# Odd mixer: the HGRN2 gate product right behind the latent queries, and the HGRN2 half of the closing product ahead of the GLA transposes

## The chip, the cores and the metric

One core of a Trainium2 chip runs the whole program. The metric is device time in microseconds. The kernel before takes 1820.97 us (median of 3 runs, 1820.81 to 1821.23). The core's engines are TensorE (PE, with its weight loads as PEld), VectorE (DVE), ScalarE (ACT), GpSimd (POOL) and SyncE (SP), whose queue issues nearly all DMAs.

## The reference

A backbone of two layers for 256 latent tokens of width 1024, with a context of 256 tokens that runs through the same weights. Layer 0 mixes by FFT and by a long convolution; layer 1, the odd layer, by two chunked linear-attention scans: GLA in raster order and HGRN2 in column order, each in both directions. Around the mixer stand two SwiGLU FFNs; each sub-layer is modulated and closed by `x <- LN(alpha*x + gate*f(x))`. The change is in the odd mixer, cut here to what matters:

```python
u = h @ w_in                    # qc kc vc rc af ab | qd ffl fbl idd gd
lat_gla, lat_hg, r, g = features(h);  ctx_gla, ctx_hg, rc, gc = features(hc)
o_gla, _ = _scan_two_way(lat_gla, ctx_gla, False)
o_hg, _ = _scan_two_way(tuple(to_col(a) for a in lat_hg), ctx_hg, False)
yg = _rms_heads(o_gla, gla_g) * silu(r)
yh = _rms_heads(from_col(o_hg) * sigmoid(g), hg_g)
y = concatenate([yg, yh]) @ w_out
```

`g`, the HGRN2 readout gate, is one product of the latent tokens with 512 columns of `w_in`. `y @ w_out` sums over eight feature blocks: in the kernel's order the first four are HGRN2's, the last four GLA's.

## The kernel before, in words

Tokens stand in four tiles of 128: 0 and 1 latent, 2 and 3 context. The features of all four, transposed and split in a high and a low fp32r part, are the eight tiles `hT`. A weight unit of 128 x 1024 floats comes by one DMA into a `raw` slot (three slots); ScalarE casts its high part (L78), VectorE subtracts the low part (L79), and TensorE does three products, high by high, low by high and high by low. The class `Stream` (L41 to L91) does this a few units ahead; `queue_odd` (L1111) lists the mixer's units in the order of use, and `g_(name, default)` reads the table of numbers G0 (L97).

No scheduler orders the work: each engine runs its instructions in the order in which the Python program records them. Between groups of matmuls the program calls `step(n)`, which records n pieces of the background queue `bg`; `flush()` records all of it. `due(t)` records the late transposes, modulation and split of token tile t for `hT` (normalisation `xn` at L398, transposes `ptr` at L411, modulation `hm` at L430, casts `hT` at L226).

In `odd_mixer` (L1119) come, in this order:

- Six latent query products in `fm_lat` (L1147): four of HGRN2 (`qh`, L1160) and two of GLA (`qg`, L1169), of 24 matmuls of 256 columns each. `due(2)` stands after the first, `flush()` behind the fourth, `due(3)` after the fifth.
- The low-rank decay product `pab` (L1183) with all four token tiles, and the feature-major units of forget gates and keys for all tokens.
- `tm_group` (L1408): the token-major products V1 and then V0, each 4 weight units by 4 token tiles, so 16 tile units with a `step(1)` behind each. During V0 `states` (L1316) of HGRN2 pair 1 run: transposes `pt`, `pb` (L1324), their copies `kT` (L1327), and two pieces later the products `pu` (L1339). `scores` (L1352) with masking by `copy_predicated` (L1372) and the sum `am` (L1376), and `outputs` (L1379) into `OH` and `OG`, follow.
- The readout gate `gg`: a `tm_group` of 2 token tiles, 8 tile units with `step(2)` behind each, which carries the scores and outputs of HGRN2 pair 2 as its filler. `permute` (L1417) brings it to column order by DMA.
- `readout(0, 4)` (L1486): the GLA gate `rc` of tile 0 with four pieces per unit, then Silu, the products `rg` by the norm's gain, `flush()`, and then `norm_og(0)`, the transposes of `OH` in `to_yt` (L1506) and of `OG` tile 0 in `og_yt(0)` (L1516).
- `close_latents` (L1628): the closing product of tile 0, k = 0 to 7 with two halves of three matmuls (L460 to L462) and `step(1)` after each k; then `readout(1, 1)`, the OG half of tile 1, and the rest.

Of the kernel before, what the change touches and what calls it, by code (L numbers as in the profile page):

```python
# [18 lines left out]
P = 128  # L19
D = 1024  # L20
KD = D // P
# [81 lines left out]
def g_(n, d):  # L103
    SEEN[n] = G0.get(n, d)
    return G.get(n, G0.get(n, d))
# [23 lines left out]
def kernel(ctx: ExitStack, tc: tile.TileContext, a, out, stop=None):  # L129
# [14 lines left out]
    def S(shape, dt=F32, name="s"):  # L144
        count[0] += 1
        return sp.tile(shape, dt, tag="s", name=f"{name}{count[0]}")
# [9 lines left out]
    def PS(name="ps"):  # L156
        count[0] += 1
        return ps.tile([P, 512], F32, tag="ps", name=f"{name}{count[0]}")
# [7 lines left out]
    def step(n=1):  # L166
        for _ in range(n):
            while bg:
                try:
                    next(bg[0])  # L170
                    break
                except StopIteration:
                    bg.pop(0)

    def flush():
        while bg:
            step()

    def run(*gens):
        for g in gens:  # L180
            for _ in g:
                pass

    def run_some(g, n):
        for _ in range(n):
            next(g, None)

    def chain(*gens):
        for g in gens:
            yield from g  # L190

    def zipped(*gens):
        gens = list(gens)
        while gens:
            for g in list(gens):
                try:
                    next(g)
                except StopIteration:
                    gens.remove(g)
            yield  # L200
# [253 lines left out]
    def due(t):  # L454
        if t in pend:
            run(pend.pop(t))
# [71 lines left out]
    def tm_mm(y, w, kp, t):  # L528

        for kk in range(2):  # L530
            k = 2 * kp + kk
            c = slice(512 * kk, 512 * kk + 512)
            x = hT[k][:, :, P * t:P * t + P]
            for n in range(2):
                pe.matmul(y, lhsT=x[:, n], rhs=w[0][:, c], start=n + k == 0, stop=False)
        for kk in range(2):
            k = 2 * kp + kk
            pe.matmul(y, lhsT=hT[k][:, 0, P * t:P * t + P], rhs=w[1][:, 512 * kk:512 * kk + 512], start=False, stop=k == KD - 1)
# [571 lines left out]

    def queue_odd():  # L1111
        for f in range(17):
            ws.add(a["od_fm"][f], f != 6, f < g_("SPN", 4), g_(f"qoi{f}", int(f in (1, 3, 4) or f > 5 and f % 2 == 1)))
        for n in range(4):
            for kp in range(4):
                ws.add(a["od_tm"][n, kp], True, n == 3, g_(f"qot{n}{kp}", kp % 2))
        for k in range(KD):
            ws.add(a["od_out"][P * k:P * k + P, :], True, k < 5, g_(f"qoo{k}", int(k < 5)))

    def odd_mixer():  # L1120
# [26 lines left out]
        def fm_lat(n):  # L1147
# [6 lines left out]
            step(n)  # L1154
            return o

        qs = S([P, 4, L], name="qh")
        for i in range(4):
            o = fm_lat(g_(f"o{i}", 2))
            act.copy(scan_view(qs[:, i]), raster(o))  # L1160
            if i == g_("od2", 0):
                due(2)
            if i == g_("of", 3):
                flush()
        q[1], q[2] = qs[:, 0:2], qs[:, 2:4]
        q[0] = S([P, 2, L], name="qg")
        for i in range(2):
            o = fm_lat(2)
            act.activation(q[0][:, i], o, AF.Copy, scale=0.125)  # L1169
            due(3)  # L1170
        az = []
        for i in range(2):
            z = S([P, 2, 512], name="az")
# [229 lines left out]
        def attend(j, tt):  # L1403
            yield from scores(j, tt)
            yield
            yield from outputs(j, tt)

        def tm_group(tiles, n):  # L1408
            y = {t: PS("tm") for t in tiles}
            for kp in range(4):  # L1410
                w = ws.get()
                for t in tiles:
                    tm_mm(y[t], w, kp, t)
                    step(n)
            return y

        def permute(dst, src):  # L1417
            for r in range(4):
                for w in range(2):
                    p0 = 64 * (r % 2) + 32 * w  # L1420
                    sy.dma_start(out=dst[r:P:4, w, :], in_=src[p0:p0 + 32, r // 2, :])


        bg.extend([zipped(operands(0, j), operands(1, j)) for j in (1, 2)])
        y = tm_group(range(NT), 1)
# [7 lines left out]
        OG = S([P, 2, 512], name="OG")  # L1433
        OH = S([P, 2, 512], name="OH")
        bg.append(zipped(operands(0, 0), operands(1, 0)))
        for j in (1, 2):
            bg.append(zipped(states(0, j), states(1, j)))
            bg.extend([attend(j, tt) for tt in range(2)])
        y = tm_group(range(NT), 1)
        gl_, gc_ = (S([P, 2, 512], name="vg") for _ in range(2))  # L1440
        for t in range(2):
            act.copy(gl_[:, t], y[t])
# [22 lines left out]
        def norm_og(t):  # L1465
            return norm_heads(OG, t, lambda h: rg[:, t, P * h:P * h + P])

        bg.extend([scores(0, 0), zipped(states(0, 0), states(1, 0)), scores(0, 1), outputs(0, 0)])
        y = tm_group(range(2), 2)
        gg = S([P, 2, 512], name="gg")  # L1470
        for t in range(2):
            act.copy(gg[:, t], y[t])
        gq = S([P, 2, 512], name="gp")
        permute(gq, gg)

        def hg_gate(tt):
            act.activation(gq[:, tt], gq[:, tt], AF.Tanh, scale=0.5)
            yield
            dve.tensor_scalar(gq[:, tt], gq[:, tt], 0.5, 0.5, op0=ALU.mult, op1=ALU.add)
            dve.tensor_tensor(OH[:, tt], OH[:, tt], gq[:, tt], op=ALU.mult)  # L1480
            yield

        rest = list(bg)
        bg.clear()
        bg.append(zipped(chain(*rest), chain(zipped(*[chain(hg_gate(t), norm_heads(OH, t, lambda h: gn[:, 1])) for t in range(2)]))))
        w = {}  # L1486

        def readout(t, n):

            y = PS("rc")  # L1490
            for kp in range(4):
                if kp not in w:
                    w[kp] = ws.get(ws.pos + 4 - kp)
                tm_mm(y, w[kp], kp, t)
                step(n)
            act.activation(rg[:, t], y, AF.Silu)
            dve.tensor_tensor(rg[:, t].rearrange("p (h v) -> p h v", h=4), rg[:, t].rearrange("p (h v) -> p h v", h=4),
                              gn[:, 0:1].to_broadcast([P, 4, P]), op=ALU.mult)

        readout(0, 4)  # L1500
        ws.split_to(ws.pos + 2)
        flush()
        Y = [S([P, 2, 2, L], F32R, name="yt") for _ in range(4)]

        def to_yt(k, o):

            for f in range(2):
                pt = PS("pt")
                for tt in range(2):
                    pe.transpose(pt[:, P * tt:P * tt + P], o[:, tt, P * (k + f):P * (k + f) + P], ident)  # L1510
                yh, yl = Y[k // 2][:, f, 0], Y[k // 2][:, f, 1]
                act.copy(raster(yh), scan_view(pt[:, 0:L]))
                dve.tensor_tensor(raster(yl), scan_view(pt[:, 0:L]), raster(yh).bitcast(F32), op=ALU.subtract)
                yield
# [7 lines left out]
                split(y[:, :, 0], y[:, :, 1], pt[:, 256 * n:256 * n + 256].rearrange("p (f t) -> p f t", f=2))  # L1522
            yield

        run(norm_og(0), to_yt(0, OH), to_yt(2, OH), og_yt(0))

        def rest():

# [1 line left out]
            w.clear()  # L1530
            hT.clear()

        return Y, outputs(0, 1), rest, chain(norm_og(1), iter([None] * 3)), og_yt(1)


    def queue_ffn_lat(l, i):
        for c in range(11):
# [87 lines left out]
                [slice(0, 512), slice(512, 768), slice(768, 1024)])  # L1625
        flush()

    def close_latents(Y, out1, rest, norm1, yt1, nxt):  # L1628


        ln = []
        run(load_ln(ln, 1, 1, GATE_ROW[1, 5], 1))
        g, b, gates = ln
        first = ws.pos
        limit = first + KD
        while limit < len(ws.units) and ws.units[limit][2]:
            limit += 1
        w, y = {}, {t: [PS("y"), PS("y")] for t in range(2)}

        def mm(t, k, h):  # L1640
            hh, hl = (Y[k // 2][:, k % 2, i, P * t:P * t + P] for i in range(2))
            c = slice(512 * h, 512 * h + 512)
            mm3(y[t][h], hh, hl, w[k][0][:, c], w[k][1][:, c], k == 0, k == KD - 1)

        bg.append(out1)
        for k in range(KD):
            w[k] = ws.get(limit)
            for h in range(2):
                mm(0, k, h)
            step(1)  # L1650
            ws.split_to(first + (4, 5, 6, 7, 7, 8, 9, 9)[k])
        flush()
        key[0] = "m1"
        bg.append(close(0, y[0], gates[0], g, b, ALPHA, EPS, nxt, True))
        rest()
        run(norm1)
        for i, (h, k) in enumerate([(h, k) for h in range(2) for k in range(4)]):
            mm(1, k, h)
            if i % 2:
                step(1)  # L1660
                ws.split_to(first + 10 + i // 2)
        run(yt1)
        for i, (h, k) in enumerate([(h, k) for h in range(2) for k in range(4, 8)]):
            mm(1, k, h)
            if i % 2:
                step(1)
        flush()
        bg.append(close(1, y[1], gates[0], g, b, ALPHA, EPS, nxt, True))
        step(1)
# [336 lines left out]
```

## Time and profile before

| | us |
|---|---|
| median of 3 runs | 1820.97 (1820.81 to 1821.23) |
| the profiled execution, whole | 1818.72 |
| its span | 1816.9 |
| TensorE busy in the span | 1735.9 (96%) |
| VectorE busy | 1253.7 (69%) |
| ScalarE busy | 716.6 (39%) |
| GpSimd busy | 254.7 (14%) |
| HBM read | 308.38 MB, 172 GB/s over the span |

The mean granted TensorE clock is 0.983. The profile is of one execution on one core: busy times are sums over instructions, the span is from the first instruction to the last. The busy shares are averages over stages with different limits; a wait is read in its stage. The odd mixer lies at about 1370 to 1640 us of the span.

### The profile page before, as it was taken

Reading aid. Unit: us, or ns where it says so; the run is one execution under the profiler, and the core shown is the slowest. Engines: PE = TensorE matmul, PEld = TensorE weight load, DVE = VectorE, ACT = ScalarE, POOL = GpSimd, SP = SyncE. Lnnn points to the kernel's source line nnn. Section 1 sums busy time; section 2 is a strip of 40 time slices with the busy share of each in tenths; the row PEclk is TensorE's granted clock in tenths of the full one; section 3 lists DMA queues with packets and bytes.
Section 4 is the critical chain, followed back from the end, with each engine's and each line's share of the span. In section 5 each row is a group of like instructions: output and inputs, shape, how many; then the busy total and the mean of one; then the engine's idle time right before and its main releaser. Section 6 shows DMA issues by size and latency. Waiting matters only on the chain. (4 is left out here: it accounts for less than half of the span.)

```text
span 1816.9 us, 21949 instructions
## 1 busy us (share of the span) xinstructions
PE 1735.9 (96%) x8212; PEld 1406.3 (77%) x8212; DVE 1253.7 (69%) x1819; ACT 716.6 (39%) x1049; POOL 254.7 (14%) x273
## 2 busy tenths in 40 slices
PE   7999999999999999999999999999998999869998
PEld 5788888877766788888887788888877778647887
DVE  6688887687688777676477677743577594656756
ACT  5532223453323442332335423333355463344443
POOL 1323311011000111111001111111011250110000
PEclk9999999999999999999999999999999999889999
DMA  9545765653124055554655455435554223535664
GB/s 330 211 180 198 254 236 213 239 177 132 71 74 158 24 201 213 188 186 173 221 187 168 165 216 201 174 102 199 197 178 145 93 82 108 162 114 208 212 211 135
DMA packets 91595, 315.10 MB, mean 173 GB/s; under 512 B 10849, under 2 KB 11585, under 8 KB 91489
## 3 DMA queue, kind: packets, MB, share of 16 engines
q1 hardware_dynamic: 86048, 297.29, 47.0%
q0 software_dynamic: 4576, 15.91, 2.7%
q8 instruction: 64, 1.05, 0.2%
q10 hardware_dynamic: 864, 0.51, 0.1%
q14 instruction: 43, 0.34, 0.1%
HBM read 308.38 MB, written 4.24 MB: 172 GB/s over the span
## 5 line engine op out<-in xcount | busy, mean ns | idle before, releaser
L79 DVE TENSOR_TENSOR wlo<-raw,whi 128x1024 fp32r<-128x1024 f32 x331 | 415.4, 1259 | 305.1 <-ACT whi L78 297.8
L78 ACT CAST whi<-raw 128x1024 fp32r<-128x1024 f32 x331 | 345.3, 1051 | 268.5 <-PE y L494 97.9
L243 DVE SCALAR_TENSOR_TENSOR mt<-mraw,cb 128x1024 bf16<-128x1024 f32 x256 | 309.6, 1249 | 3.0 <-DMA mraw<-in_mod_w_dram 3.0
L469 PE MATMUL pu<-hT,whi 128*128 128x512 f32 x1152 | 274.3, 390 | 0.0
L469 PEld LDWEIGHTS pu<-hT,whi 128*128 128x128 f32 x1152 | 215.8, 188 | 46.5 <-issue 1.0
L494 PE MATMUL y<-whi,hh 128*128 128x512 f32 x924 | 229.8, 390 | 2.9 <-ACT whi L78 2.9
L469 PE MATMUL pa<-hT,whi 128*128 128x512 f32 x960 | 228.3, 390 | 0.0
L469 PEld LDWEIGHTS pa<-hT,whi 128*128 128x128 f32 x960 | 179.6, 188 | 38.4 <-issue 0.9
L494 PEld LDWEIGHTS y<-whi,hh 128*128 128x128 f32 x924 | 172.5, 188 | 40.4 <-ACT whi L78 5.0
L226 ACT CAST hh<-sa 128x256 fp32r<-128x256 f32 x120 | 42.8, 404 | 312.1 <-DVE sa L640 312.1
L227 POOL TENSOR_TENSOR hh<-sa,hh 128x256 fp32r<-128x256 f32 x120 | 86.3, 740 | 515.9 <-ACT hh L226 484.6
L469 PE MATMUL pu<-hT,wlo 128*128 128x512 f32 x576 | 142.4, 389 | 0.4 <-DVE wlo L79 0.4
L469 PEld LDWEIGHTS pu<-hT,wlo 128*128 128x128 f32 x576 | 108.0, 188 | 23.2 <-DVE wlo L79 0.8
L494 PE MATMUL y<-wlo,hh 128*128 128x512 f32 x462 | 124.5, 391 | 0.2
L469 PE MATMUL pa<-hT,wlo 128*128 128x512 f32 x480 | 118.6, 389 | 0.0
L234 POOL TENSOR_TENSOR rstd<-rp,mhalf 128x1 f32<-128x1 f32 x42 | 36.5, 873 | 507.6 <-DVE rp L233 504.6
L79 DVE TENSOR_TENSOR lo<-raw,hi 128x1024 fp32r<-128x1024 f32 x63 | 80.4, 1290 | 38.5 <-ACT hi L78 37.9
L469 PEld LDWEIGHTS pa<-hT,wlo 128*128 128x128 f32 x480 | 90.1, 188 | 18.7
L494 PEld LDWEIGHTS y<-wlo,hh 128*128 128x128 f32 x462 | 86.6, 188 | 19.3 <-DVE wlo L79 1.5
L640 DVE TENSOR_TENSOR sa<-sa,pu 128x512 f32<-128x512 f32 x60 | 41.0, 683 | 58.0 <-PE pu L469 37.4
L78 ACT CAST hi<-raw 128x1024 fp32r<-128x1024 f32 x63 | 64.9, 1053 | 29.4 <-DMA raw<-in_ffn_out_dram 17.3
L562 PE MATMUL hd<-hi,hT 128*128 128x512 f32 x256 | 68.3, 416 | 6.5 <-ACT hT L226 3.7
(412 smaller groups left out, 2301.7 us busy)
## 6 DMA issues: line engine op xcount, KB each, us to landing
raw<-in_ffn_out_dram SPq DMA_DIRECT2D x154, 512.0 KB, 4.2
mraw<-in_mod_w_dram SPq DMA_DIRECT2D x144, 512.0 KB, 5.1
raw<-in_ffn_in_dram SPq DMA_DIRECT2D x120, 512.0 KB, 3.8
raw<-in_ffn_tm_dram SPq DMA_DIRECT2D x44, 512.0 KB, 3.3
raw<-in_od_fm_dram SPq DMA_DIRECT2D x17, 512.0 KB, 3.4
raw<-in_od_tm_dram SPq DMA_DIRECT2D x16, 512.0 KB, 3.3
raw<-in_ffn_head_dram SPq DMA_DIRECT2D x12, 512.0 KB, 4.6
raw<-in_ev_in_dram SPq DMA_DIRECT2D x12, 512.0 KB, 3.3
```

The costliest lines, as they stand in the source:

```text
L78: self.nc.scalar.copy(hi, w)
L79: self.nc.vector.tensor_tensor(lo, w, hi.bitcast(F32), op=ALU.subtract)
L226: act.copy(dst_hi, src)
L227: (lo_eng or dve).tensor_tensor(dst_lo, src, dst_hi.bitcast(F32), op=ALU.subtract)
L234: gp.tensor_tensor(dst, t, mhalf.to_broadcast([P, n]), op=ALU.pow)
L243: dve.scalar_tensor_tensor(H([P, D], BF16, "mt"), w, 1.0, cb[s], op0=ALU.mult, op1=ALU.mult, accum_out=acc[:, s, b:b + 1])
L469: pe.matmul(o, lhsT=w[a_][:, P * k:P * k + P], rhs=view(hT[k][:, b_, :]), start=n + k == 0, stop=n == 2 and k == KD - 1)
L494: pe.matmul(y[t][i], lhsT=lhs(k, t)[a_], rhs=w[b_][:, cols[t][i]], start=k + a_ + b_ == 0, stop=k == nk - 1 and b_ == 1)
L562: pe.matmul(y[u // 4], lhsT=hT[k][:, order[p_][0], P * t:P * t + P], rhs=w[u][order[p_][1]][:, 512 * kk:512 * kk + 512], start=p_ == 0 and ...
L640: dve.tensor_tensor(sa, sa, pu, op=ALU.mult)
```

## The change

Three edits. First, `queue_odd` lists the readout gate's four units right behind the six query units, and its product, copies and `permute` are recorded there. `due(2)` moves behind the `flush()` after the third query, `due(3)` behind the gate. Second, V0 takes one piece and two pieces of background work by turns (24 pieces for 16 units); HGRN2 attention that is left then runs out with nothing between (`while left[0]: step()`). Third, `readout` gets `between`: the flush, two pieces of `norm_og(0)` and the transposes of `OH` are recorded before Silu; the rest of `norm_og(0)` runs at the start of `close_latents`, the transposes of `OG` tile 0 at k = 4, and `step(k > 1)` takes no piece at k = 0 and 1. Table lookups for unused numbers go.

```diff
     def queue_odd():
         for f in range(17):
-            ws.add(a["od_fm"][f], f != 6, f < g_("SPN", 4), g_(f"qoi{f}", int(f in (1, 3, 4) or f > 5 and f % 2 == 1)))
-        for n in range(4):
+            if f == 6:
+                for kp in range(4):
+                    ws.add(a["od_tm"][2, kp], True, False, 0)
+            ws.add(a["od_fm"][f], f != 6, f < g_("SPN", 4), 0)
+        for n in (0, 1, 3):
...
             act.copy(scan_view(qs[:, i]), raster(o))
-            if i == g_("od2", 0):
-                due(2)
             if i == g_("of", 3):
                 flush()
+                due(2)
...
             act.activation(q[0][:, i], o, AF.Copy, scale=0.125)
-            due(3)
+
+        y = tm_group(range(2), 2)
+        gg = S([P, 2, 512], name="gg")
+        for t in range(2):
+            act.copy(gg[:, t], y[t])
+        gq = S([P, 2, 512], name="gp")
+        permute(gq, gg)
+        due(3)
...
         for j in (1, 2):
             bg.append(zipped(states(0, j), states(1, j)))
-            bg.extend([attend(j, tt) for tt in range(2)])
-        y = tm_group(range(NT), 1)
+            bg.extend([counted(attend(j, tt)) for tt in range(2)])
+        y = tm_group(range(NT), lambda n: 1 + n % 2)
...
-        bg.extend([scores(0, 0), zipped(states(0, 0), states(1, 0)), scores(0, 1), outputs(0, 0)])
-        y = tm_group(range(2), 2)
-        gg = S([P, 2, 512], name="gg")
-        for t in range(2):
-            act.copy(gg[:, t], y[t])
-        gq = S([P, 2, 512], name="gp")
-        permute(gq, gg)
-
+        def split_ahead():
+
+            ws.split_to(len(ws.units) - N_LAT - KD + 1)
+            yield
+
+        bg.extend([scores(0, 0), zipped(states(0, 0), states(1, 0)), scores(0, 1), split_ahead(), outputs(0, 0)])
...
+        while left[0]:
+            step()
         rest = list(bg)
...
-        def readout(t, n):
+        def readout(t, n, between=None):
...
                 step(n)
+            if between:
+                between()
             act.activation(rg[:, t], y, AF.Silu)
...
-        readout(0, 4)
-        ws.split_to(ws.pos + 2)
-        flush()
...
-        run(norm_og(0), to_yt(0, OH), to_yt(2, OH), og_yt(0))
+        norm0 = norm_og(0)
+
+        def between():
+            flush()
+            run_some(norm0, 2)
+            run(to_yt(0, OH), to_yt(2, OH))
+
+        readout(0, 4, between)
...
+        run(norm0)
         bg.append(out1)
         for k in range(KD):
             w[k] = ws.get(limit)
+            if k == 4:
+                run(yt0)
             for h in range(2):
                 mm(0, k, h)
-            step(1)
-            ws.split_to(first + (4, 5, 6, 7, 7, 8, 9, 9)[k])
+            step(k > 1)
+            if k > 3:
+                ws.split_to(first + k + 2)
```

Line numbers of the new kernel differ from the old ones by about 14 to 24 from `fm_lat` on. Three places show how the instructions move.

On ScalarE between the first query's copy and the weight cast for the sixth query (`whi_10824`), the kernel before has this; `xn_10644` is context tile 2, `xn_10807` tile 3, `hm` and `hT` here are tile 2's:

```order
L398 ACTIVATE xn_10644<-x_10629,nb_10645,rstd_10663 128x512 x2
L1160 COPY qh_10680<-ql_10681 128x4x64
L430 ACTIVATE hm_10725<-ptr_10715,modc 128x128 x4
L430 ACTIVATE hm_10730<-ptr_10720,modc 128x128 x4
L226 CAST hT_10398<-hm_10725 128x4x128
L226 CAST hT_10398<-hm_10730 128x4x128
L1160 COPY qh_10680<-ql_10739 128x4x64
L78 CAST hi_10776<-raw_10651 128x1024
L1160 COPY qh_10680<-ql_10773 128x4x64
L317 ACTIVATE dev_10812,ss_10811<-x_10770,nm_10809 128x1024
L398 ACTIVATE xn_10807<-x_10770,nb_10808,rstd_10814 128x512 x2
L78 CAST whi_10824<-raw_10657 128x1024
```

The changed kernel has:

```order
L398 ACTIVATE xn_10644<-x_10629,nb_10645,rstd_10663 128x512 x2
L1178 COPY qh_10680<-ql_10681 128x4x64
L1178 COPY qh_10680<-ql_10715 128x4x64
L78 CAST hi_10752<-raw_10651 128x1024
L1178 COPY qh_10680<-ql_10749 128x4x64
L317 ACTIVATE dev_10788,ss_10787<-x_10746,nm_10785 128x1024
L398 ACTIVATE xn_10783<-x_10746,nb_10784,rstd_10790 128x512 x2
L430 ACTIVATE hm_10807<-ptr_10797,modc 128x128 x4
L430 ACTIVATE hm_10812<-ptr_10802,modc 128x128 x4
L226 CAST hT_10398<-hm_10807 128x4x128
L226 CAST hT_10398<-hm_10812 128x4x128
L78 CAST whi_10824<-raw_10657 128x1024
```

The modulation and split of tile 2 have moved from before the normalisation of tile 3 to behind it, directly ahead of the sixth query's weight cast.

On TensorE in V0, around the states of HGRN2 pair 1, the kernel before has, from the third tile unit of the second weight unit back to the second of it and on to the products `pu`:

```order
L1324 MATMUL pt_11730<-ident,kc_11504 128x128 x2
L1325 MATMUL pb_11731<-ident,kc_11504 128x128
L1324 MATMUL pt_11730<-ident,kc_11504 128x128 x2
L1325 MATMUL pb_11731<-ident,kc_11504 128x128
L535 MATMUL tm_11623<-whi_11554,hT_10398 128x512 x4
L538 MATMUL tm_11623<-wlo_11555,hT_10398 128x512 x2
L535 MATMUL tm_11624<-whi_11554,hT_10398 128x512 x4
L538 MATMUL tm_11624<-wlo_11555,hT_10398 128x512 x2
L535 MATMUL tm_11621<-whi_11627,hT_10398 128x512 x4
L538 MATMUL tm_11621<-wlo_11628,hT_10398 128x512 x2
L1339 MATMUL pu_11765<-v_11605,kT_11727 128x128 x2
L1340 MATMUL pu_11765<-v_11606,kT_11727 128x128
```

The changed kernel has, from the last unit of the first weight unit on:

```order
L1348 MATMUL pt_11798<-ident,kc_11590 128x128 x2
L1349 MATMUL pb_11799<-ident,kc_11590 128x128
L1348 MATMUL pt_11798<-ident,kc_11590 128x128 x2
L1349 MATMUL pb_11799<-ident,kc_11590 128x128
L535 MATMUL tm_11707<-whi_11640,hT_10398 128x512 x4
L538 MATMUL tm_11707<-wlo_11641,hT_10398 128x512 x2
L535 MATMUL tm_11708<-whi_11640,hT_10398 128x512 x4
L538 MATMUL tm_11708<-wlo_11641,hT_10398 128x512 x2
L1363 MATMUL pu_11827<-v_11691,kT_11795 128x128 x2
L1364 MATMUL pu_11827<-v_11692,kT_11795 128x128
```

Before, `pt` and `pb` follow the sixth of V0's units and `pu` the ninth; now they follow the fourth, and `pu` the sixth.

On TensorE behind the readout of tile 0, the kernel before has the transposes of `OH`, of `OG`, and the first closing product:

```order
L1510 MATMUL pt_12290<-ident,OH_11620 128x128 x2
L1510 MATMUL pt_12295<-ident,OH_11620 128x128 x2
L1510 MATMUL pt_12300<-ident,OH_11620 128x128 x2
L1510 MATMUL pt_12305<-ident,OH_11620 128x128 x2
L1519 MATMUL pt_12310<-ident,OG_11619 128x128 x4
L460 MATMUL y_12325<-hi_12258,yt_12274 128x512
L461 MATMUL y_12325<-lo_12259,yt_12274 128x512
L462 MATMUL y_12325<-hi_12258,yt_12274 128x512
L460 MATMUL y_12326<-hi_12258,yt_12274 128x512
```

The changed kernel goes from the transposes of `OH` straight on, here k = 0 and the start of k = 1:

```order
L1524 MATMUL pt_12278<-ident,OH_11706 128x128 x2
L1524 MATMUL pt_12283<-ident,OH_11706 128x128 x2
L1524 MATMUL pt_12288<-ident,OH_11706 128x128 x2
L1524 MATMUL pt_12293<-ident,OH_11706 128x128 x2
L460 MATMUL y_12306<-hi_12232,yt_12089 128x512
L461 MATMUL y_12306<-lo_12233,yt_12089 128x512
L462 MATMUL y_12306<-hi_12232,yt_12089 128x512
L460 MATMUL y_12307<-hi_12232,yt_12089 128x512
L461 MATMUL y_12307<-lo_12233,yt_12089 128x512
L462 MATMUL y_12307<-hi_12232,yt_12089 128x512
L460 MATMUL y_12306<-hi_12238,yt_12089 128x512
```

The four transposes of `OG` (one row, x4) now stand between k = 3 and k = 4 of that product.

## Rows read from the trace of the kernel before

**Rows 1.** Waits of TensorE, 1367 to 1640 us: us in total, times, longest

```profile
PE y L460 <- ACT yt L226: 10.2, 1, 10.2
PE pt L1519 <- DVE OG L1460: 8.1, 2, 7.0
PE ptr L411 <- ACT xn L398: 5.6, 1, 5.6
PE pu L1339 <- ACT kT L1327: 2.3, 1, 2.3
```

**Rows 2.** Windows: stretch, us, busy (instructions) of five engines, PEclk, DMA share, GB/s

```profile
1376.00:1378.00 2.00, 1.50 (x7) 1.50 (x8) 1.93 (x4) 1.95 (x4) 0.00 (x0) 0.50 1.04 392
1560.14:1565.80 5.66, 5.66 (x22) 4.47 (x22) 2.73 (x9) 0.74 (x2) 1.10 (x3) 0.50 0.98 279
1612.00:1616.00 4.00, 2.48 (x6) 1.99 (x7) 3.41 (x6) 3.88 (x7) 2.45 (x2) 0.70 0.01 2
```

**Rows 3.** Timeline of TensorE, front: start us, us, instruction, [idle before, releaser]

```profile
1376.50 1.97 PE L411 MATMUL ptr<-ident,xn 128*128 128x128 f32 x8 [5.63 <-ACT xn L398]
1391.96 1.20 PE L1153 MATMUL ql<-hT,whi 128*128 128x256 f32 x8
1395.07 3.64 PE L1183 MATMUL pab<-hT,raw 128*32 128x512 f32 x32
```

**Rows 4.** Timeline of VectorE, front

```profile
1367.85 1.28 DVE L347 SCALAR_TENSOR_TENSOR z<-z,mv,lng 128x1024 f32<-128x1024 f32 x1
1378.95 0.69 DVE L338 BATCH_NORM_STATS2 st<-z 128x6 f32<-128x512 f32 x1
1381.76 0.20 DVE L342 BATCH_NORM_AGGREGATE mv<-st 128x2 f32<-128x12 f32 x1
1382.07 2.02 DVE L347 SCALAR_TENSOR_TENSOR z<-z,mv,lng 128x1024 f32<-128x1024 f32 x1
```

**Rows 5.** Timeline of ScalarE, front, the last row in V0

```profile
1377.71 2.90 ACT L430 ACTIVATE hm<-ptr,modc 128x128 f32<-128x128 f32 x8
1380.47 1.18 ACT L226 CAST hT<-hm 128x512 fp32r<-128x512 f32 x2
1389.20 1.53 ACT L398 ACTIVATE xn<-x,nb,rstd 128x512 f32<-128x512 f32 x2 [1.04 <-DVE nb L388]
1390.63 1.04 ACT L78 CAST whi<-raw 128x1024 fp32r<-128x1024 f32 x1
...
1492.70 0.89 ACT L1294 ACTIVATE w<-G 128x256 f32<-128x256 f32 x2
```

**Rows 6.** Timeline of TensorE, V0 to the second readout

```profile
1495.06 0.71 PE L1339 MATMUL pu<-v,kT 128*128 128x128 f32 x4 [2.26 <-ACT kT L1327]
...
1552.10 1.04 PE L1510 MATMUL pt<-ident,OH 128*128 128x128 f32 x8
...
1579.31 1.08 PE L535 MATMUL rc<-hi,hT 128*128 128x512 f32 x4
...
1580.68 1.07 PE L535 MATMUL rc<-hi,hT 128*128 128x512 f32 x4
```

**Rows 7.** Timeline of VectorE, HGRN2's attention to the closing product

```profile
1526.25 0.90 DVE L1372 COPY_PREDICATED az<-masks,pF 128x256 f32<-128x256 int32 x2
1527.18 0.42 DVE L1376 TENSOR_TENSOR am<-az 128x256 f32<-128x256 f32 x1
...
1538.23 1.45 DVE L1372 COPY_PREDICATED az<-masks,pF 128x256 f32<-128x256 int32 x4 [1.41 <-PE pF L1364]
...
1550.03 0.69 DVE L1376 TENSOR_TENSOR am<-az 128x512 f32<-128x512 f32 x1
...
1554.23 3.50 DVE L79 TENSOR_TENSOR lo<-raw,hi 128x1024 fp32r<-128x1024 f32 x3 [0.24 <-ACT hi L78]
```

**Rows 8.** Timeline of ScalarE, Silu of the first readout

```profile
1551.37 1.28 ACT L1496 ACT_TABLE_LOAD   x1
1552.67 0.60 ACT L1496 ACTIVATE rg<-rc 128x512 f32<-128x512 f32 x1
```

More of the change, by code (lines that the diff above doesn't have):

```diff
@@ L1112, in queue_odd @@
         for f in range(17):
-            ws.add(a["od_fm"][f], f != 6, f < g_("SPN", 4), g_(f"qoi{f}", int(f in (1, 3, 4) or f > 5 and f % 2 == 1)))
-        for n in range(4):
+            if f == 6:
[3 more added lines that the diff above has]
+        for n in (0, 1, 3):
             for kp in range(4):
-                ws.add(a["od_tm"][n, kp], True, n == 3, g_(f"qot{n}{kp}", kp % 2))
+                ws.add(a["od_tm"][n, kp], True, n == 3, 0)
         for k in range(KD):
@@ L1155, in fm_lat, with tm_group, permute @@
             return o
+        def tm_group(tiles, n):
+            y = {t: PS("tm") for t in tiles}
+            for kp in range(4):
+                w = ws.get()
+                for t in tiles:
+                    tm_mm(y[t], w, kp, t)
+                    step(n(len(tiles) * kp + t) if callable(n) else n)
+            return y
+        def permute(dst, src):
+            for r in range(4):
+                for w in range(2):
+                    p0 = 64 * (r % 2) + 32 * w
+                    sy.dma_start(out=dst[r:P:4, w, :], in_=src[p0:p0 + 32, r // 2, :])
         qs = S([P, 4, L], name="qh")
@@ L1406, in attend @@
             yield from outputs(j, tt)
[L1408 to L1421, printed above, removed]
         bg.extend([zipped(operands(0, j), operands(1, j)) for j in (1, 2)])
@@ L1435, in odd_mixer, with counted @@
         bg.append(zipped(operands(0, 0), operands(1, 0)))
+        left = [4]
+        def counted(g):
+            yield from g
+            left[0] -= 1
         for j in (1, 2):
             bg.append(zipped(states(0, j), states(1, j)))
-            bg.extend([attend(j, tt) for tt in range(2)])
-        y = tm_group(range(NT), 1)
+            bg.extend([counted(attend(j, tt)) for tt in range(2)])
+        y = tm_group(range(NT), lambda n: 1 + n % 2)
         gl_, gc_ = (S([P, 2, 512], name="vg") for _ in range(2))
@@ L1531, in rest @@
             hT.clear()
-        return Y, outputs(0, 1), rest, chain(norm_og(1), iter([None] * 3)), og_yt(1)
+        return Y, norm0, og_yt(0), outputs(0, 1), rest, chain(norm_og(1), iter([None] * 3)), og_yt(1)
+    N_LAT = 44 + KF
     def queue_ffn_lat(l, i):
@@ L1626, in ffn_lat, with close_latents @@
         flush()
-    def close_latents(Y, out1, rest, norm1, yt1, nxt):
+    def close_latents(Y, norm0, yt0, out1, rest, norm1, yt1, nxt):
         ln = []
```

## The prediction

> **What bounds the kernel now.** I read the page's busy times first: TensorE works 1735.9 of 1816.9 us, so the span is TensorE's work plus its waits and the stretches at a lower clock. I then read TensorE's waits in the odd mixer: four matter, of 10.2, 7.0 (the larger of two that make 8.1), 5.6 and 2.3 us [rows 1]. Every one ends on ScalarE or VectorE. After the 5.63 us wait the granted clock is 0.50, half of full speed, that is 1.2 instead of 2.4 GHz [rows 2, 3]; after the 7.0 us wait it is 0.50 for 5.66 us [rows 2]. The 2.26 us wait ahead of `pu` [rows 6] left no such row. So each of these two waits cost its length and about 2.5 us again, since some 5 us behind it ran at half speed. The change moves work across all but the 10.2 us wait, which ends at `y`'s half for tile 1 with the same instructions around it in both kernels; I leave it as it is.
>
> Nothing is taken out of TensorE's work. The prediction is therefore four places where waits come, go or move.
>
> **Front: the sixth query, +5.8.** `pab` ends at 1395.07 + 3.64 = 1398.7 [rows 3] and reads all four tiles; its end is my mark. Before, TensorE waits 5.63 us for tile 2's `xn`, from 1370.87 to 1376.50 [rows 3]. With `due(2)` behind the flush, the second and third queries fill that wait. What is late next is tile 3. Four queries (1391.96 to 1395.07 is one: 3.11 us [rows 3]) and the tile-2 transposes of about 0.9 bring TensorE from 1370.87 to 1384.2, and then it needs the sixth query's weights.
>
> These weights' high part is cast by ScalarE. Before, the cast (1390.63) follows tile 3's `xn` (1389.20, 1.53) directly [rows 5]. In the changed order tile 2's `hm` and `hT` stand between. First, `xn` of tile 3 comes earlier: VectorE's aggregate ran at 1381.76 though its statistics were done at 1378.95 + 0.69 = 1379.64, because tile 2's work stood ahead; and the `z` behind it took 2.02 where another took 1.28 [rows 4]. That is 2.1 + 0.7, about 3.0 with the pieces between. So `xn` ends near 1387.7 instead of 1390.7. Then come `hm` 2.90 and `hT` 1.18, less overlap 3.94, and the cast of 1.04 [rows 5]: the sixth query starts at about 1392.65, 0.7 later than before. Its idle time is one piece now: 1384.2 to 1392.65, 8.4 us, more than the 5.63 and 7.0 behind which the clock was at half. I price the slow stretch at 2.2 to 2.5 us, as there. Then the gate's eight tile units run, 8 x 1.36 = 10.9 us at the pace of one unit (1580.68 - 1579.31 = 1.37 [rows 6]); their weights come one by one in the time of two units and I see no stall. Then comes tile 3's `hT`, which `pab` needs: four `hm` and two `hT` casts are half of the 2.90 and 1.18 [rows 5], about 2.1 us, that no matmul covers, since `due(3)` now stands directly ahead of `pab`. Tile 3's transposes (0.8) leave their old place. Sum at `pab`'s end: 10.9 moved, plus 0.7, plus 2.9 for the clock and the spread of the stretch over the gate, plus 2.15: 16.7 later, so 5.8 net of the moved work. Bounds: 3.7 without a slow stretch, 7 with a longer one.
>
> **V0: `pu`, +3.1 wait and +2.5 clock.** Twice the background pieces mean that `pt` follows V0's fourth unit instead of its sixth, and `pu` its sixth instead of its ninth. TensorE arrives three units earlier: 3 x 1.36 = 4.1 us. But ScalarE's `kT` copies cannot come sooner than the last `w` exponential, 1492.70 + 0.89 = 1493.6 [rows 5]; before, one weight cast stood between, about 1 us. So `pu` starts at about 1494.1, not 1495.06 [rows 6], 1.0 earlier, where TensorE is 4.1 earlier: the wait grows from 2.26 to 5.4. That is close to the front's 5.63, behind which the clock was at half, and 5 us at half speed cost 2.5. Bounds: 0.6 (the exponentials move forward too, no clock loss) to 6.
>
> **HGRN2 pair 2 without filler, +3.0.** Before, the gate's units stand between `scores` and `outputs` of that pair; now `while left[0]: step()` records them back to back. `outputs` needs `am`, which follows masking 0.90 and the sum 0.42 [rows 7]: 1.3 us without anything on TensorE, twice; 0.4 more for the shorter distances around `kT` of pair 0. The gate product was the cover, and it has gone to the front. Bounds: 0 (two scores are issued ahead of two outputs) to 4.
>
> **Tail, -5.2.** Before, from `OH`'s transposes (1552.10) to the end of the closing product (1579.31) are 27.2 us [rows 6]. Its work at full speed is 48 products at 1.37 / 6 = 0.228 us, 11.0, and 36 small matmuls at 0.11, a little under `OH`'s 1.04 for eight [rows 6], 4.0: 15.0. The other 12.2 are the 7.0 us wait for `OG` [rows 1], the slow stretch behind it [rows 2] and some waits for weights. The changed order has `OH`'s half first. I see three smaller waits. One: the first product needs `yt`'s low part. VectorE is busy without a gap from the masking at 1538.23 to the sum at 1550.03 + 0.69 [rows 7], 12.5 us; one weight's low part more, then two more (1.17 each, 3.50 / 3 [rows 7]), a reduction and `yt` itself make about 17.2 where TensorE has 15.1 of work from the same masking; the handshakes of square and reduction add a microsecond: 3.2. Two: the third unit's cast now stands behind Silu's table load and Silu, 1.28 + 0.60 [rows 8]; with its low part 1.17 and two products of 0.69 on VectorE that is 4.4, against 12 products, 2.7: 1.5. Three: `OG`'s transposes at k = 4, 0.5, with a weight cast ahead (1.04), a `yt` cast and low part of 0.4 each: 2.3. Each is shorter than the two waits that brought half clock. After: 15.0 + 3.2 + 1.5 + 2.3 = 22.0, so 5.2 less. Bounds: 12.2 less (no waits) to nothing gained.
>
> **Sum.** 5.8 + 5.6 + 3.0 - 5.2 = 9.2. The profiled execution took 1818.72, which gives 1827.9; it lies 2.25 below the median of the runs, 1820.97, so the median to expect is 1830.2.
>
> **Two rules of the Trainium skill.** On the clock the rows say: half after waits of 5.63 and 7.0, not after 2.26; yet between 1612 and 1616, with only short waits, the mean was 0.70 [rows 2]. The Trainium skill, "TensorE: Matmul & The Clock Gate", section "HAM oscillation — how this bites in real kernels", says that a kernel which waits again and again returns the engine to the low clock each time. By that rule the tail's three waits would bring a slow stretch of their own; this is the first rival. On queue order the rows show VectorE's aggregate for tile 3 held for 2.1 us, though its input was ready, by tile 2's operations recorded ahead of it [rows 4]. The same page of the Trainium skill, section "Architectural detail: the array is 16× 32×32, not 1× 128×128", says that ScalarE and VectorE take their queues strictly in order; the trace agrees with its 2.1 us, and it speaks against the third rival.
>
> **Rivals.** First, clock: the tail's short waits or the pair without filler bring half clock, as the 0.70 row allows. One stretch costs 2.5, two 5: 9.2 + 4 gives about 1834. Against it speaks the 2.26 wait at full clock.
>
> Second, relief, the side of not slower: ScalarE and VectorE lose the late casts, low parts and copies of the gate, four of each kind and two copies, from their densest stretch. If they are then never late in the attention and the tail, the masking's 1.3 us waits vanish and the tail gains the whole 12.2. With the front and V0 as forecast: 5.8 + 5.6 + 0 - 12.2 = -0.8, so 1820. It decides if the three tail waits together are under about 2 us. VectorE's 12.5 us without a gap, which are not the gate's, speak against it.
>
> Third, faster: in addition the front does not wait on ScalarE's order, as when the sixth query's weights were cast before tile 2's `hm`. Then the 5.63 wait and its slow stretch go: -4.9 at the front instead of 5.8, and with V0's cost halved and the tail free the sum is about -11.5: 1809.5. The recorded order of ScalarE speaks against it, since the cast stands behind `hT`.
>
> Fourth, the change does not do what it says: waits only change places, each shortened one appears as another of the same length, 1821.
>
> **How the numbers follow.** The forecast has 0.45, the clock rival 0.15, relief 0.22, faster 0.13, no effect 0.05. The likeliest time is 1830.2, its own range 1825 to 1834. A difference under 0.2%, 3.6 us, can't be told from none: same is 1817.3 to 1824.6. Faster gets the third rival and a bit, 0.14. Same gets most of relief and the fourth, less what of relief falls on either side, 0.21. Slower gets 0.65. The range is 1817.3 to 1836: it reaches over relief, and leaves out the third rival and a clock loss of two stretches in more places than the tail.
>
> **What would show it.** In the new trace, step by step: one TensorE wait of about 8 us ahead of the sixth query, ended by ScalarE's weight cast, with a clock of 0.50 behind it, and one of about 2 us ahead of `pab`, ended by `hT`; a wait of about 5.4 us ahead of the first `pu`, ended by `kT`, again with 0.50 behind it; two of about 1.3 us ended by `am`; no 7.0 us wait for `OG`, but some 3.2, 1.5 and 2.3 us ended by `yt` or weights' low parts; the 10.2 us wait as it was. The prediction is wrong if the sixth query starts without a long wait, if `pu`'s wait stays near 2 us, or if the tail from `OH`'s transposes to the end of the closing product takes 15 to 17 us.

## The result, and the profile after

The changed kernel takes 1837.16 us (median of 4 runs, 1832.15 to 1839.85) against 1821.1 for the kernel before: 1.0082 times the time, interval 1.0066 to 1.0099. It is slower, as forecast, but by 16 us instead of 9.2, and 1.2 us beyond the range. Its profiled execution took 1839.85, span 1837.7, so the two profiled spans lie 20.8 apart.

TensorE's waits of the changed kernel from 1367 to 1605 us, in the columns of [rows 1]:

```profile
PE ql L1156 <- ACT whi L78: 7.8, 1, 7.8
PE y L460 <- ACT yt L226: 5.4, 1, 5.4
PE pu L1363 <- ACT kT L1351: 4.9, 1, 4.9
PE po L1410 <- DVE am L1400: 2.2, 2, 1.1
PE pab L1207 <- ACT hT L226: 2.1, 1, 2.1
PE y L462 <- DVE yt L1527: 1.8, 1, 1.8
PE y L461 <- DVE lo L79: 1.5, 2, 1.2
```

Five are the forecast's, at the forecast's place and nearly its size: 7.8 (8.4) ahead of the sixth query, 2.1 ahead of `pab`, 4.9 (5.4) at `pu`, two of 1.1 on `am` (1.3). The 7.0 and 5.6 us waits of [rows 1] are gone. New against the forecast is the second row: 5.4 us in the closing product, on `yt`, where I had 2.3. The clock behind the waits, windows in the columns of [rows 2]:

```profile
1396.45:1401.70 5.25, 5.25 (x24) 5.25 (x25) 3.81 (x3) 2.55 (x4) 2.14 (x3) 0.50 0.48 154
1416.08:1421.30 5.22, 5.22 (x33) 1.19 (x33) 2.50 (x3) 1.41 (x2) 0.00 (x0) 0.68 0.49 144
1516.60:1522.00 5.40, 5.33 (x25) 5.34 (x26) 5.40 (x15) 2.35 (x6) 5.40 (x4) 0.52 0.04 15
1592.30:1597.00 4.70, 4.54 (x10) 3.15 (x11) 3.56 (x5) 2.37 (x4) 0.00 (x0) 0.51 0.70 223
```

Half clock stands behind the sixth query's, `pu`'s and `yt`'s waits, and 0.68 behind the 2.1 us one: `pab` took 5.2 us instead of the 3.6 of [rows 3].

The next table cuts every profiled execution at the same five TensorE starts: the first latent query, the first `pf` behind `pab`, the first V1 product, `OH`'s transposes, the second readout. "Front" holds the gate's 10.9 us where it is early (E), "V1 to OH" where it is late (L). From that first `pf` to V1 all take 58.1.

| run | gate | median | first query at | front | V1 to OH | OH to readout | rest |
|---|---|---|---|---|---|---|---|
| before | L | 1821.1 | 1367.8 | 30.8 | 95.4 | 27.2 | 237.6 |
| changed | E | 1837.16 | 1372.0 | 49.3 | 93.9 | 27.0 | 237.4 |
| r1_before_again | L | 1820.91 | 1368.2 | 30.5 | 95.3 | 27.1 | 237.2 |
| r0_changed_again | E | 1836.66 | 1371.1 | 49.0 | 93.9 | 27.3 | 237.3 |
| a1_old_dues | E | 1833.00 | 1371.6 | 42.1 | 94.2 | 26.7 | 238.9 |
| a2_v0_one_piece | E | 1833.14 | 1371.2 | 46.0 | 89.7 | 27.7 | 238.2 |
| a3_og_first | E | 1836.97 | 1374.5 | 47.5 | 91.4 | 24.7 | 238.6 |
| d1_cast_ahead | E | 1833.14 | 1374.1 | 45.2 | 94.2 | 27.0 | 237.6 |
| d2_gate_back | L | 1835.96 | 1372.0 | 38.3 | 108.9 | 23.5 | 237.0 |
| b3_gate_alone | E | 1828.35 | 1370.7 | 42.1 | 90.8 | 26.6 | 238.2 |
| b1_tail_alone | L | 1819.30 | 1368.9 | 30.9 | 95.3 | 26.5 | 238.1 |
| c1_tail_og_first | L | 1818.18 | 1372.3 | 30.1 | 95.4 | 23.1 | 238.3 |
| c2_tail_and_early_rows | L | 1812.34 | 1372.1 | 30.4 | 95.3 | 19.0 | 239.7 |
| c4_tail_and_due | L | 1812.80 | 1371.1 | 29.4 | 97.0 | 19.0 | 238.1 |
| c3_changed_tail_mended | E | 1828.17 | 1372.9 | 46.0 | 94.0 | 20.1 | 237.6 |
| e1_gate_front_rest_mended | E | 1822.15 | 1372.3 | 42.6 | 91.4 | 20.1 | 238.0 |

Before to changed, with the gate's 10.9 taken to its new place: front +7.6, V1 to OH +9.4, tail -0.2, and 4.2 ahead of the first query, in work that the change does not touch. Without the last it is 16.6, close to the medians' 16.1.

One trace does not fix such a place: with the same TensorE instructions the changed front takes 46.0 to 49.3 (changed, r0, a2, a3, c3) and the changed stretch from V1 to `OH` 91.4 to 94.2 (changed, r0, a1, a3, c3, d1). The waits there agree within 0.3; what differs is the clock behind them. The old front, by contrast, takes 30.1 to 30.9 in five traces.

### The profile page after: what moved, and what is told of

It reads as the page before. It is cut to its first block, busy times and chain, and to the rows that moved or that the text cites. A ratio compares the mean times of both kernels' runs of the same rounds, so it can differ in the third digit from the quotient of the medians.

```text
span 1837.7 us, 21954 instructions
## 1 busy us (share of the span) xinstructions
PE 1743.6 (95%) x8212; PEld 1410.9 (77%) x8212; DVE 1253.6 (68%) x1819; ACT 716.4 (39%) x1049; POOL 252.5 (14%) x273
```

## The experiments

**The changed kernel and the kernel before again.** No edit.

> The changed kernel once more, in the same company as the three below. In its first trace 4.2 us of the 20.8 us between the spans had come up before the first moved instruction, in work that both kernels have in the same order. Theory A (that part is chance: the clock falls for longer or shorter behind the same short waits of layer 0 in one execution and another): this trace has another offset at the first latent query, somewhere between 0 and 5 us, and the times spread over several us again; the part from the first query to the end of the span is 16.6 us over that of before, within 3 us. Theory B (the changed program slows layer 0): the offset is 4.2 us again, and the spread is as small as before's 1.4 us.

> The kernel before once more, for a second trace. Theory A (where the first latent query starts is chance of layer 0's clock): its first query starts somewhere from 1366 to 1374 us, not at 1367.8 again; from that query to the end it is within 2 us of the first trace's 449.1 us. Rival B (the changed program slows layer 0): 1367.8 within 0.5 us.

Measured: the second trace of the changed kernel agrees with the first within 0.3 us in every stretch behind the first query. The 4.2 us ahead of it became 3.2; over all traces the first query starts between 1367.8 and 1374.5, also in c1, c2 and c4, which have before's order up to there (1371.1 to 1372.3). Before's second trace gave 1368.2, within rival B's 0.5 us, and its times went from 1818.16 to 1824.57. So the offset is not the gate's move, and I don't count it; whether chance or the programs' memory layout sets it stays open.

**Front: the late features back.** `due(2)` behind the first query, `due(3)` behind the fifth, gate still early.

```diff
+            if i == 0:
+                due(2)
             if i == g_("of", 3):
                 flush()
-                due(2)
...
             act.activation(q[0][:, i], o, AF.Copy, scale=0.125)
+            due(3)
...
         permute(gq, gg)
-        due(3)
```

(`flush()` stands behind the third query in both kernels; the outline of the kernel before has it behind the fourth.)

> Changed kernel with the late features of tiles 2 and 3 back where they were, behind the first and the fifth query; the gate product stays at the front. Theory A (the front costs because tile 2's modulation and split stand on ScalarE ahead of the sixth query's weight cast, and tile 3's directly ahead of pab): the waits of 7.8 and 2.1 us with their slow clock go, one of 5.6 us for tile 2's xn comes back, and the time is about 7.6 us less than the changed kernel's. Rival B (the gate's four units at the front cost by themselves, through their casts, low parts or loads): at most 2 us less.

Measured: front 42.1, of which 10.9 are the gate, so 0.4 over before; the only wait left in it:

```profile
PE ptr L411 <- ACT xn L398: 5.3, 1, 5.3
```

The stretch gives back 7.2 against the changed kernel's first trace and 3.9 against the shortest of the same front; the median gives back 3.7. Rival B falls by the stretch: with the gate's units still early it is within 0.4 of before, so the moved `due` calls made the rest. In whole times a1, a2 and d1 (1.0062, 1.0069 and 1.0071 of before) lie below the changed kernel (1.0082, again 1.0086), but the intervals, some 0.002 either way, overlap: the traces give the sizes of these three steps, the times only their sign.

**Front: the cast ahead of tile 2's modulation.**

```diff
                 flush()
+                ws.split_to(ws.pos + 2)
                 due(2)
```

> Changed kernel with the sixth query's weight cast recorded ahead of due(2), so ahead of tile 2's modulation and split on ScalarE. Theory A (the 7.8 us wait is the queue order on ScalarE): the wait falls by the 3.9 us of hm and hT to about 3.9 us and the slow clock behind it is shorter or gone; the front takes 43 to 45 us instead of 46 to 49, the whole 4 to 6 us less than the changed kernel. Rival B (tile 3's normalisation ends last there, the order only names it): the wait stays over 6 us.

Measured: the wait is 4.0, shorter by the 3.8 between the ends of `xn` and `hT`; front 45.2, median 3.5 less. In the changed kernel ScalarE's rows, to be laid beside [rows 5], are these:

```profile
1390.13 1.52 ACT L398 ACTIVATE xn<-x,nb,rstd 128x512 f32<-128x512 f32 x2 [1.04 <-DVE nb L388]
1391.55 2.88 ACT L430 ACTIVATE hm<-ptr,modc 128x128 f32<-128x128 f32 x8
1394.29 1.16 ACT L226 CAST hT<-hm 128x512 fp32r<-128x512 f32 x2
1395.32 1.08 ACT L78 CAST whi<-raw 128x1024 fp32r<-128x1024 f32 x1
```

`hm` and `hT` fill the time from `xn` to the cast; with that row ahead of them the wait ends 3.8 sooner. The queue's order made half of it, tile 3's normalisation the other half.

**Attention: V0 with one piece per unit.**

```diff
-        y = tm_group(range(NT), lambda n: 1 + n % 2)
+        y = tm_group(range(NT), 1)
```

> Changed kernel with one background piece behind each V0 unit, as before. Theory A (the doubled pace brings TensorE to the first state products 3 units early, where kT can't be earlier): the 4.9 us wait falls back to about 2.3 us and the clock of about 0.6 behind it goes, together 5 us; more of HGRN2's attention is left over to run without filler, with one or two more waits of 1.1 us on am; in all 3 us less than the changed kernel. Rival B (what costs in this stretch is the missing filler): no less, or up to 3 us more.

Measured: V1 to OH 89.7, 4.2 less; median 3.5 less. Waits of that stretch:

```profile
PE po L1410 <- DVE am L1400: 3.3, 3, 1.1
PE pu L1363 <- ACT kT L1351: 2.2, 1, 2.2
```

`pu`'s wait is before's again, one more `am` wait stands. Without the gate's 10.9 the stretch of before is 84.5, so 5.2 is left over. The `am` waits, 3.3 of it, are the ones that before does not have; I put the whole to the missing filler.

**The gate alone, and the gate put back.** First the kernel before with only the gate moved (and the HGRN2 attention that is left recorded without filler), then the changed kernel with only the gate at its old place. The lines are in b3 as in the changed kernel; in d2 the units and the product are in before's place and the last loop is gone.

```diff
+            if f == 6:
+                for kp in range(4):
+                    ws.add(a["od_tm"][2, kp], True, False, 0)
...
+        y = tm_group(range(2), 2)
...
+        while left[0]:
+            step()
```

> The kernel before with the gate's units and product at the front, the late features of tiles 2 and 3 where they were, V0 with one piece per unit, and the old tail; the HGRN2 attention left over runs without filler. Theory A (moving the gate takes the cover from attention and costs nothing at the front): front 0 to 0.5 us over the gate's own 10.9; from V1 to OH's transposes 5 us more than before without the gate, in three waits of 1.1 us on am and shorter ones; in all 4 to 6 us slower. Rival B (the engines are relieved late, as in my second rival): within 1 us of before.

> Changed kernel with the gate's units and product back behind V0 as the filler of HGRN2's attention; the late features stay behind the third query and ahead of pab, V0 keeps its doubled pace, the tail is the new one. Theory A (the gate's move itself costs its cover in attention and nothing at the front): front 37 to 39 us, 7 over before; from V1 to OH's transposes about 5 over before's 95.4, all at pu, without waits on am; 3 to 5 us less than the changed kernel. Rival B (the doubled pace alone makes the cost of attention): 9 over in that stretch, the same time as the changed kernel.

Measured: b3 is 1.0041 of before (interval 1.0026 to 1.0056), front 0.4 over its 10.9, V1 to OH 6.4 over, with three `am` waits of 1.1 and one of 0.9 on `st`. That is theory A, dearer than it said: 1.0041 is 7.5 us, not 4 to 6. d2 missed both expectations in the stretch: 13.6 over, not 5 or 9. Its time is the changed kernel's, as rival B said, but by another road. No `am` wait is left, but TensorE waits 7.17 for `OH` ahead of its transposes, and ScalarE's tanh waits for the gate from `permute`:

```profile
1577.29 0.47 PE L1518 MATMUL pt<-ident,OH 128*128 128x128 f32 x1 [7.17 <-DVE OH L1465]
```

```profile
1565.80 0.63 ACT L1486 ACTIVATE gp<-gp 128x512 f32<-128x512 f32 x1 [4.67 <-DMA gp<-gg]
```

Before, `permute` starts at 1531.8, 20.3 us ahead of `OH`'s transposes. Here it starts at 1558.9, and TensorE's other work ends 11.2 us later; that does not cover the gate's own way to `OH`: copies, `permute`, tanh, product, norm. That V0's double pace makes this, by using the filler up ahead of the gate, is my reading; no run has the late gate and the double pace apart from the rest of the change. So an early gate does buy something, though only where V0's pace makes a late one dear. I had not seen this.

**The tail alone.** The kernel before with the third edit only; its DMA order is before's, instruction by instruction.

> The kernel before with the third edit alone: readout(0) with the flush, the first pieces of norm_og(0) and OH's transposes ahead of Silu, the HGRN2 half first, OG's transposes at k = 4. The stretch from OH's transposes to the second readout was 27.2 us before and 26.7 to 27.7 us in the changed kernel and two variants. Theory A (OG's cast and the late weights behind it give the time back): 26 to 28 us again, the whole time within 1 us of before. Rival B, as I had forecast it (waits of 3.2, 1.5 and 2.3 us, no slow clock): 22 us, 5 us faster than before.

Measured: 26.5, median 1819.30, 0.9991 of before (0.9982 to 1.0001). Theory A, with 1.6 us less than before where it said within 1, and an interval that reaches no change. The one 7.0 us wait became these, 6.0 together:

```profile
PE y L460 <- ACT yt L226: 3.8, 1, 3.8
PE y L461 <- DVE lo L79: 1.7, 1, 1.7
PE y L462 <- DVE yt L1523: 0.5, 1, 0.5
```

**The tail's two mends.** a3 is the changed kernel with the first, c1 the tail alone with the first, c2 with both.

```diff
         for k in range(KD):
-            w[k] = ws.get(limit)
             if k == 4:
                 run(yt0)
+            w[k] = ws.get(limit)
```

```diff
+        run(load_ln(ln_lat, 1, 1, GATE_ROW[1, 5], 1))
         readout(0, 4, between)
...
-        ln = []
-        run(load_ln(ln, 1, 1, GATE_ROW[1, 5], 1))
-        g, b, gates = ln
+        g, b, gates = ln_lat
```

> Changed kernel with GLA's transposes and their casts recorded ahead of the weight split at k = 4, so that ScalarE casts yt before the two weight units that land late. Theory A (queue order: the 5.4 us wait is the two late weight casts ahead of yt's on ScalarE): that wait shrinks to about 1 us; the units behind still land as late, so k = 5 waits up to 3 us for its low part; the clock may stay up; 1.5 to 3 us less than the changed kernel. Rival B (the late weights alone bound it): the same time, with the wait moved to k = 5.

> The tail alone, with OG's transposes and casts ahead of the weight split at k = 4, and the row broadcasts where they were. Against the tail alone (26.5 us from OH's transposes to the second readout) and with both mends (19.0 us). Theory A (the broadcasts beside the closing weights bound it): 22 to 25 us, with one wait of 2.5 to 4 us for weights. Rival B (cast order alone made the wait): 19 to 21 us.

> The tail alone, with two mends: OG's transposes and casts ahead of the weight split at k = 4, and the three row broadcasts (norm gain, norm bias, gate; 1.57 MB) issued ahead of the first readout rather than beside the closing weights, whose loads took 8.7 us to land there. Theory A (cast order and the crowded DMA make the 5.4 us wait): the stretch takes 20 to 23 us, no wait over 2.5 us in it, clock near 1.00; 4 to 7 us faster than before. Rival B (the raw slots, freed by VectorE's low parts, bound the loads): waits of 3 us or more for weights stay, 25 us or more.

Measured: the stretch goes from 26.5 to 23.1 by the order and to 19.0 by the early rows too; in the changed kernel from 27.0 to 24.7 by the order, though its median did not move. Nor do whole times show the order by itself on the tail alone: c1's 1818.18 is 0.9988 of before (0.9978 to 0.9997), beside b1's 0.9991. Its longest wait in the stretch is 1.7, where theory A had 2.5 to 4. c2's median is 1812.34, 0.9956 of before (0.9941 to 0.9971): it beats both kernels, and by more than its theory A. In its stretch the clock is full; c1 comes second, the kernel with the tail alone third:

```profile
1555.94:1574.94 19.00, 16.30 (x86) 12.11 (x84) 13.88 (x21) 11.29 (x17) 1.01 (x1) 1.00 0.60 194
```

```profile
1555.85:1578.96 23.11, 19.39 (x85) 14.50 (x84) 13.85 (x21) 11.18 (x17) 2.63 (x4) 0.85 0.72 242
```

```profile
1553.26:1579.79 26.53, 20.43 (x85) 15.27 (x84) 13.96 (x21) 11.28 (x17) 2.63 (x4) 0.81 0.72 236
```

VectorE and ScalarE do the same work in all three (13.9 and 11.2 to 11.3 us); what differs is TensorE's clock and idle time, and the transfers beside them. Of the 4.1 us from c1 to c2, 3.1 are TensorE's busy time, 19.39 against 16.30 at 0.85 and 1.00 of the clock, and 1.0 is idle time.

**On c2: due(2) behind the second query.** The line `if i == 0:` ahead of `due(2)` becomes `if i == 1:`.

> The tail with both mends, and due(2) behind the second query instead of the first, so that the second query covers 2.9 us of the 5.6 us wait for tile 2's xn, while tile 2's modulation still comes ahead of tile 3's normalisation on ScalarE. Theory A: that wait falls to about 2.7 us, the slow clock behind it (2.3 us) shrinks or goes, and the front takes 26 to 28 us instead of 30.5: 3 to 5 us less than the tail with both mends. Rival B (tile 3's features come as late as the sixth query and pab need them): the same wait comes back ahead of the sixth query, no gain.

Measured: the wait for `xn` falls to 2.53, a second of 0.90 comes at tile 3; front 29.4, 1.0 less, not the 2.5 to 4.5 of theory A. The wait moved in part, as rival B had it. Another 1.7 are lost in V1 to OH, behind a wait at `pu` that is as long as c2's, with a clock of 0.72 over 6 us where c2 has 1.00; that they come from the edit is not shown. 1812.80 against 1812.34: no gain.

**Do the terms add up?** The changed kernel with both mends of the tail; and c2 with nothing but the gate moved to the front.

> Changed kernel with both mends of the tail (OG's casts ahead of the weight split, row broadcasts ahead of the first readout). Theory A (the places add up, and the tail's gain was there to be had): the stretch from OH's transposes to the second readout takes 19 to 21 us instead of 27, the time is 6 to 9 us less than the changed kernel's 1837, and still 6 to 10 us over before, by the front and attention. Rival B (the tail in the changed kernel is held by VectorE, later against TensorE without the gate's units): 23 us or more.

> The tail with both mends, old places of the late features, one piece per V0 unit, and the gate at the front: what is left of the change is the gate's place and the new tail. Theory A (additive): 5 to 7 us over the kernel with both mends and the gate late, so 1817 to 1820, all of it between V1 and OH's transposes, in three waits of 1.1 us on am and what the clock loses behind them. Rival B (the gate's casts at the front free ScalarE and VectorE late, which the mended tail can now use): 1812 to 1815.

Measured: c3's tail takes 20.1, and its median is 1828.17, 9 less than the changed kernel and 1.0047 of before (1.0031 to 1.0064). e1 is 1822.15, 9.8 over c2 and 1.0003 of before (0.9993 to 1.0013), which makes 8.6; both are more than expected: V1 to OH 7.0 over, front 1.2, tail 1.1. The gate's place alone costs all that the mended tail gains.

## Why the prediction was wrong

**The step that failed is the tail, and in it the third wait.** I forecast 5.2 us gained, with 2.3 for `OG`'s `yt` at k = 4; the gain was 0.2 and the wait 5.4, with half clock for another 4.7 us behind it. My working allowed one weight cast of 1.04 ahead of `yt` on ScalarE. There were two, and they waited for data. ScalarE of the changed kernel:

```profile
1589.75 1.04 ACT L78 CAST whi<-raw 128x1024 fp32r<-128x1024 f32 x1 [4.09 <-DMA raw<-in_od_out_dram]
1590.99 1.04 ACT L78 CAST whi<-raw 128x1024 fp32r<-128x1024 f32 x1 [0.20 <-DMA raw<-in_od_out_dram]
1591.94 0.36 ACT L226 CAST yt<-pt 128x256 fp32r<-128x256 f32 x1
```

`OG`'s transposes start at 1586.39; their cast stands behind two weights that land late. The weight loads from 1560 to 1605 us, from issue to landing:

```profile
DMA to landing us min/median/max: 3.1/3.8/8.7
```

In c2 the longest is 5.6. GpSimd issues three row broadcasts, 1.57 MB in all, from 1577.84 on, between these loads. In the kernel before they go out from 1559.56 on, behind three weight loads, and the next weight load follows at 1570.08; none issued from 1555 to 1575 took over 4.6. I had priced the order on ScalarE and VectorE and took the weights as present, because before they came during the 7.0 us wait. That wait was the weights' cover, and I removed it without asking what else it hid. The two mends on the tail alone show both halves in the traces: the cast's order 3.4 us, the broadcasts 4.1, the clock included. Whole times confirm the two together, not the first alone.

The tail's other terms missed as well, and cancelled by luck. The stretch before and in the changed kernel:

```profile
1552.10:1579.31 27.21, 18.58 (x85) 14.09 (x84) 15.34 (x22) 12.97 (x20) 2.63 (x4) 0.81 0.62 196
```

```profile
1573.28:1600.30 27.02, 18.31 (x86) 13.56 (x85) 15.70 (x23) 11.48 (x17) 2.63 (x4) 0.87 0.70 221
```

The work that I put at 15.0 takes 16.3 at full clock (c2), 1.3 more. The first two waits took 2.1 and 1.2 instead of 3.2 and 1.5, 1.4 less, though the second's own terms in the forecast give 1.7. What is left, 5.0, is the third wait, 3.1 more, and 2.0 of slow clock (18.31 against 16.30).

The other steps:

- Front, 5.8 forecast, 7.6 measured here, and 4.3 to 7.6 over the five traces with this front. The mechanism was right: the wait, its releaser, the 2.1 us on `hT`. Two terms were missing. Tile 3's transposes, 1.0 us, stand ahead of that wait and nothing covers them either; and I had no slow stretch behind 2.1 us, since none stood behind the 2.26 of [rows 6]. Yet the kernel before held the case: the 0.70 from 1612 to 1616 of [rows 2] stands around a 2.10 us wait ahead of `hd`, and behind it the clock is 0.50. `pab` ran 5.2 us in four of seven traces with this wait and 3.6 in three. First the changed kernel, then the kernel before:

```profile
1412.95 1.03 PE L411 MATMUL ptr<-ident,xn 128*128 128x128 f32 x8
1416.08 5.26 PE L1207 MATMUL pab<-hT,raw 128*32 128x512 f32 x32 [2.10 <-ACT hT L226]
```

```profile
1613.53 6.67 PE L562 MATMUL hd<-hi,hT 128*128 128x512 f32 x21 [2.10 <-ACT hT L226]
```

```profile
1614.00:1616.00 2.00, 2.00 (x6) 1.52 (x6) 1.48 (x2) 1.88 (x2) 2.00 (x2) 0.50 0.02 4
```

- V0, 5.6 forecast: 4.9 instead of 5.4 at `pu`, and 0.52 clock for 5.4 us behind it. Right in this trace. Taken back alone it gave 4.2.
- No filler, 3.0 forecast: `am` waits of 2.2, and 0.67 of the clock for 5.1 us behind the first of them, 1.7 more. The place comes to some 4, and to 5.2 to 7.0 where V0 runs at its old pace (a2, b3, e1). The slow stretch in the changed kernel, and a window around both `am` waits in a3:

```profile
1548.90:1554.00 5.10, 4.94 (x28) 4.80 (x28) 0.57 (x2) 0.37 (x1) 0.00 (x0) 0.67 0.00 0
```

```profile
1545.00:1557.00 12.00, 9.83 (x98) 9.39 (x97) 4.69 (x13) 4.02 (x8) 0.00 (x0) 1.00 0.01 1
```

- Attention together: 8.6 forecast, 9.4 measured, 6.9 in a3's trace of the same instructions.
- The first rival, short waits that bring slow clock, holds at `pab` in four traces of seven and at `am` in the changed kernel, while a3 has 1.00 over both of its `am` waits. The page of the Trainium skill, "TensorE: Matmul & The Clock Gate", section "HAM oscillation — how this bites in real kernels", has a kernel that waits again and again back at the low clock after each wait; for the short waits here the traces agree with it in part. I gave the rival a price for the tail alone.
- Relief, the second rival, is refuted by b3, 7.5 us slower than before, and by e1, no faster than before and 8.6 slower than c2.
- The 10.2 us wait on tile 1's `yt` came back at its old length, as forecast.

With the tail's true size the forecast would have been 14.2, and with the front as the first trace has it 16.0. Of the 6.9 us from 9.2 to the medians' 16.1, 5.0 are the tail's.

## What to carry to other kernels

A long wait hides other lateness. Before a forecast books its removal, ask for each operand that the next work reads when it lands, the DMA ones first, and what shares the DMA then. Where a product serves as filler for a chain of short dependent steps, moving it costs the waits it covered and the clock behind them. Cast what TensorE needs next before what is only needed later and may still be in flight.

## What was unexpected of the hardware

The same 2.10 us wait ahead of `pab` left full clock in three traces (a2, a3, c3) and 0.68 in the one shown here, at the same instructions. Of loads of 512 KB whose median is 3.8 us, one took 8.7 beside broadcasts. And the work ahead of the first latent query, the same in all these programs, differs by up to 6.6 us between the traces; two traces of one program differ by 0.3 and 1.0.
